# Stored right operands of two square projections: sums formed in DRAM, ScalarE passes in a fixed order, and a later place for two products

## The chip, the cores and the metric

The kernel runs on one core of a Trainium2 chip. The metric is the device time of one execution in microseconds. A core has TensorE (PE in the profile; PEld is its weight load), VectorE (DVE), ScalarE (ACT), GpSimd (POOL) and SyncE (SP), each with its own queue of instructions that it takes in order, and 16 DMA engines that move data between DRAM and the on-chip SBUF. DMAs of this kernel are issued by SP or by POOL; only POOL issues those that add to what stands at the destination (`accum_op=ALU.add`).

## The reference

One decoder layer on x of 1024 tokens by 1024 features, all in float32:

```python
h = _layer_norm(ALPHA * h + 0.5 * _swiglu(h, ffn1_w_gate, ffn1_w_up, ffn1_w_down), ...)
mix = _token_mixers(h, w_in, ...)        # [HGRN2 recurrence ; spatial gating] @ w_out
h = _layer_norm(ALPHA * h + mix, ...)
xa = _memory_cross_attention(h, mem, ...)  # softmax(q k^T) v @ xa_w_o, 256 memory tokens
h = _layer_norm(ALPHA * h + xa, ...)
h = _layer_norm(ALPHA * h + 0.5 * _swiglu(h, ffn2_w_gate, ffn2_w_up, ffn2_w_down), ...)
```

`_swiglu` is `(silu(x @ w_gate) * (x @ w_up)) @ w_down` with an inner width of 2816. The two square matrices of this case are `w_out` (1024 x 1024, the mixers' output) and `xa_w_o` (1024 x 1024, the attention's output).

## The kernel before

Every product is made of three matmuls on operands split in two: `split` makes a hi part on ACT (a Copy that rounds) and a lo part on DVE (raw minus hi), and `mm3` (L133 to L137) multiplies hi by hi (L135), lo by hi (L136) and hi by lo (L137). Weights come through `load_split`: SP loads a raw tile (tag `raw`, three buffers, L121), ACT writes hi (L112), DVE writes lo (L113). Hi tiles have the tag `whi` with six buffers, lo tiles `wlo` with five.

The large products are done by Strassen's scheme, with seven half-size products in place of eight. In the FFNs the gate and up projections run through `st_g` and `st_u` (names end in f1 or f2 for the two FFNs; the profile writes f), then the down projection through `dp`. The two square projections are done by the class `Square`: its seven products p = 1 to 7 have on their right a block of the matrix or a sum of blocks (5 = 11+12, 6 = 5+22, 4 = 6+21, 7 = 22+12, and 1, 2, 3 are the blocks 11, 21, 22), each in two halves n of 512 KB, and each half in a hi and a lo part. These 14 right operands of each matrix are not made when they are needed. `prepare_square` makes them ahead, while the first FFN runs, and stores them in DRAM (`sq_mx` for w_out, `sq_xa` for xa_w_o), from where `Square.fetch` loads them later (`sh_` and `sl_` tiles).

Before, an operand goes through these steps: a raw tile `pre` (one buffer for all) is loaded by SP (L234), or, for a sum, POOL adds the next block from DRAM onto the same tile (L236). ACT writes hi (`ph`, L239) and its negative (`pl`, L240), POOL adds the raw tile onto `pl` by a DMA, which leaves lo (L241), SP stores hi (L242) and POOL stores lo (L243). Twelve raw tiles are loaded by SP, sixteen are accumulated.

What sets the order: the preparation is a generator (a flow) that yields numbers of microseconds. `spawn` starts a flow, and `tick(us)`, called after each piece of FFN or mixer work, lowers its count and lets it go on at zero. `prepare_square` runs from `later`, first for w_out and then for xa_w_o. The flows set the order in which the program is written; a scheduler then sets the order on each engine, and an engine keeps that order on the chip.

At the end of the token mixers there are two halves of 512 tokens (`m0`, `m1`). `body` gives the units of a half: gates and `us` units with the heads' recurrences started between them, and four `vs` units. `tail` gives four gate units (`ps_wg`); behind each the head outputs are transposed (`pt_oa`), the other group's stored result is loaded back (`mx_again`, L1231) and both are added (`s_mx`, L1047), which makes the left operand of the output projection. `msq` is that projection: products 2 (`sx2_mx`) and 1 (`sx_mx`) need only the first token half, product 7 and those after it (`sy_mx` among them) need both.

Of the kernel before, what the change touches and what calls it, by code (L numbers as in the profile page):

```python
# [20 lines left out]
HALF = T // 2  # L21
# [5 lines left out]
ALPHA = 2.0 ** 0.25  # L27
EPS = 1e-5
WARM = 32
LEVELS = [64, 32, 16, 8, 4, 2, 1]  # L30


@with_exitstack
def hybrid_layer_kernel(ctx: ExitStack, tc: tile.TileContext, a, out):
    nc = tc.nc
# [4 lines left out]
    wpool = ctx.enter_context(tc.tile_pool(name="wpool", bufs=5))  # L40
# [3 lines left out]
    dram = ctx.enter_context(tc.tile_pool(name="dram", bufs=1, space=bass.MemoryType.DRAM))  # L44
# [70 lines left out]
    def load_raw(view, name, pool=None):  # L115
        if pool is not None:
            raw = pool(f"{name}_r", [P] + list(view.shape[1:]))
            nc.sync.dma_start(raw, view)
            return raw
        raw = wpool.tile([P] + list(view.shape[1:]), F32, tag="raw", bufs=3, name=f"{name}_r")  # L120
        nc.sync.dma_start(raw, view)  # L121
        return raw

# [87 lines left out]
    def layer_norm(y, gb, bb, name):  # L211

        stt = sm(f"st_{name}", [P, 2, 6])
        for j in range(2):
# [3 lines left out]

    SUMS = {1: ["11"], 5: ["11", "12"], 6: ["11", "12", "22"], 4: ["11", "12", "22", "21"],
            2: ["21"], 3: ["22"], 7: ["22", "12"]}

    def prepare_square(w, ops, name):


        wv = w.rearrange("(kb n i p) (db d) -> kb n db p i d", kb=2, n=2, i=2, p=P, db=2)
        for n in range(2):
            raw = None
            for p, blocks in SUMS.items():  # L230
                b = wv[int(blocks[-1][0]) - 1, n, int(blocks[-1][1]) - 1]
                if len(blocks) == 1:
                    raw = wpool.tile([P, 2, HALF], F32, tag="pre", bufs=1, name=f"pre_{name}_{n}{p}")
                    nc.sync.dma_start(raw, b)  # L234
                else:
                    nc.gpsimd.dma_start(raw, b, accum_op=ALU.add)  # L236
                hi = wpool.tile([P, 2, HALF], F32R, tag="whi", bufs=6, name=f"ph_{name}_{n}{p}")
                lo = wpool.tile([P, 2, HALF], F32R, tag="wlo", bufs=5, name=f"pl_{name}_{n}{p}")
                nc.scalar.activation(hi, raw, AF.Copy)  # L239
                nc.scalar.activation(lo, hi.bitcast(F32), AF.Copy, scale=-1.0)  # L240
                nc.gpsimd.dma_start(lo, raw, accum_op=ALU.add)  # L241
                nc.sync.dma_start(ops[p - 1, n, 0], hi.bitcast(F32))  # L242
                nc.gpsimd.dma_start(ops[p - 1, n, 1], lo.bitcast(F32))  # L243
                yield 13

    class Square:

# [711 lines left out]
    class Mixers:  # L959
# [251 lines left out]
        def body(self):  # L1211
            start = [[partial(spawn_late, self.recurrence, h)] for h in range(H)]
            vs = token_units(self.half, 2560, "wvs", self.evac_v)
            return (start[0] + self.gates(1) + self.us(0) + self.us(1) + start[1] + self.gates(2)
                    + self.us(2) + self.us(3) + start[2] + self.gates(3) + vs[:2] + start[3] + vs[2:])

# [6 lines left out]
    def play(units):  # L1223
        for unit in units:
            unit()
            if not (isinstance(unit, partial) and unit.func is spawn_late):
                tick(5.2)
# [13 lines left out]
    play(m1.body())  # L1241


    msq.fetch(2, 1)
    x = msq.bank("sx2")
    for n in range(2):
# [2 lines left out]
    x = msq.bank("sx")  # L1249
    for n in range(2):  # L1250
        msq.step(1, x, 0, 0, n, True)
    play(m1.tail())
    msq.fetch(7)
    msq.gb, msq.bb = load_bc(a["ln2_g"][0], a["ln2_b"][0], "mx")
    for t in range(4):
# [179 lines left out]
```

## Time and profile before

| | before |
|---|---|
| median of 3 runs | 2135.43 us (2132.91 to 2135.46) |
| profiled execution | 2131.09 us |
| its span | 2129.3 us |
| mean granted PE clock | 0.976 |
| PE busy | 2029.2 us, 95% |
| DVE busy | 1492.0 us, 70% |
| ACT busy | 931.6 us, 44% |
| POOL busy | 166.8 us, 8% |
| q1 (SP's DMA queue) | 338.82 MB, 47.3% of 16 engines' span |
| q0 (POOL's DMA queue) | 37.75 MB, 7.9% |

The stages, by the first matmul of each: the memory's K and V projections to about 63 us, FFN1's gate and up to 553.5 us, FFN1's down to about 770 us, the mixers and their output projection to about 1245 us, cross-attention to about 1505 us, and FFN2 to the end (its gate and up to 1907.4 us). The busy time of an engine excludes its register, branch, semaphore and DMA-issuing instructions, except that POOL's DMA instructions appear in the timeline with the time that POOL spent on them. A DMA is shown by the time from its issue to its landing.

### The profile page before, as it was taken

To read this page: it belongs to the slowest core of one execution; us is meant where nothing else is said; L and a number is where in the kernel's file an instruction comes from. 1 tells how busy PE (TensorE), PEld (TensorE's weight loads), DVE (VectorE), ACT (ScalarE), POOL (GpSimd) and SP (SyncE) were. 2 spreads that over 40 slices of the span, in tenths; PEclk is the share of its full clock that TensorE was granted. 3 is DMA by queue.
4 is the path that set the end of the run, shared out by engine and by line. 5 is a ranking of instruction groups with operands and counts; after the bars stand their busy time and mean duration, and the time that the engine had idled before them with its cause. 6 is when DMAs were issued, how large, how long until landed. Compare 5 with 4: busy or idle time off the path is not lost.

```text
span 2129.3 us, 25517 instructions
## 1 busy us (share of the span) xinstructions
PE 2029.2 (95%) x9550; PEld 1688.8 (79%) x9550; DVE 1492.0 (70%) x2240; ACT 931.6 (44%) x1311; POOL 166.8 (8%) x224
## 2 busy tenths in 40 slices
PE   8999898998899999999996979999999999999998
PEld 7787686777788888888885868887888888888886
DVE  5866564756767876776773774469777677676688
ACT  6643343434443547746642434335432333334432
POOL 0111111111000220100010110002000000000011
PEclk9999899999999999999998989999999999999999
DMA  8588777877878752133225533455223233268874
GB/s 282 161 226 234 206 224 207 233 191 245 289 279 284 272 164 89 41 109 109 80 98 226 191 117 92 168 197 179 83 85 120 94 99 124 81 225 283 279 272 170
DMA packets 267420, 378.20 MB, mean 178 GB/s; under 512 B 16544, under 2 KB 156448, under 8 KB 267296
## 3 DMA queue, kind: packets, MB, share of 16 engines
q1 hardware_dynamic: 254880, 338.82, 47.3%
q0 software_dynamic: 12416, 37.75, 7.9%
q8 instruction: 75, 1.23, 0.2%
q14 instruction: 49, 0.40, 0.1%
HBM read 257.51 MB, written 104.33 MB: 170 GB/s over the span
## 4 chain that ended last, share of the span: by engine, by line
PE 68%; DVE 3%; DMA 1%; issue 1%; POOL 0%; ACT 0%; POOLq 0%; SPq 0%; DVEq 0%; ACTq 0%
PE dp_f L135 6%; PE dp_f L136 6%; PE dp_f L137 6%; PE st_uf L136 3%; PE st_gf L136 3%; PE st_gf L137 3%; PE st_uf L137 3%; PE st_uf L135 3%; PE st_gf L135 3%; PE psl L1119 2%; PE paq L135 1%; PE paq L136 1%; PE paq L137 1%; PE sx_mx L135 1%; PE ps_wu L135 1%; PE sx_mx L136 1%
## 5 line engine op out<-in xcount | busy, mean ns | idle before, releaser
L135 PE MATMUL dp_f<-wd_f_h,ah_f 128*128 128x512 f32 x552 | 209.9, 393 | 7.0 <-ACT ah_f L112 7.0
L136 PE MATMUL dp_f<-wd_f_l,ah_f 128*128 128x512 f32 x552 | 214.6, 392 | 0.2 <-DVE wd_f_l L113 0.2
L137 PE MATMUL dp_f<-wd_f_h,al_f 128*128 128x512 f32 x552 | 206.0, 390 | 0.1
L135 PEld LDWEIGHTS dp_f<-wd_f_h,ah_f 128*128 128x128 f32 x552 | 104.4, 189 | 29.3 <-ACT ah_f L112 7.8
L136 PEld LDWEIGHTS dp_f<-wd_f_l,ah_f 128*128 128x128 f32 x552 | 104.4, 189 | 22.3 <-DVE wd_f_l L113 0.7
L137 PEld LDWEIGHTS dp_f<-wd_f_h,al_f 128*128 128x128 f32 x552 | 103.6, 188 | 21.8 <-DVE al_f L113 0.5
L112 ACT ACTIVATE wd_f_h<-wd_f_r 128x1024 fp32r<-128x1024 f32 x72 | 73.2, 1021 | 94.3 <-DVE wd_f_r L587 31.7
L112 ACT ACTIVATE ah_f<-ar_f 128x1024 fp32r<-128x1024 f32 x72 | 73.4, 1020 | 67.7 <-DMA ar_f<-lops 65.5
L113 DVE TENSOR_TENSOR al_f<-ar_f,ah_f 128x1024 fp32r<-128x1024 f32 x72 | 84.5, 1174 | 23.9 <-ACT ah_f L112 23.5
L113 DVE TENSOR_TENSOR wu_f_l<-wu_f_r,wu_f_h 128x1024 fp32r<-128x1024 f32 x44 | 53.7, 1219 | 60.3 <-ACT wu_f_h L112 38.9
L113 DVE TENSOR_TENSOR wg_f_l<-wg_f_r,wg_f_h 128x1024 fp32r<-128x1024 f32 x44 | 53.6, 1219 | 56.0 <-ACT wg_f_h L112 52.7
L113 DVE TENSOR_TENSOR wd_f_l<-wd_f_r,wd_f_h 128x1024 fp32r<-128x1024 f32 x72 | 84.2, 1174 | 9.9 <-ACT wd_f_h L112 9.9
L135 PE MATMUL st_uf<-xh,wu_f_h 128*128 128x512 f32 x168 | 68.7, 409 | 17.3 <-DVE top_gf L467 14.1
L135 PE MATMUL st_gf<-xh,wg_f_h 128*128 128x512 f32 x168 | 66.8, 398 | 5.5 <-ACT wg_f_h L112 5.5
L137 PE MATMUL st_uf<-xh,wu_f_l 128*128 128x512 f32 x168 | 68.2, 406 | 1.1 <-DVE wu_f_l L113 1.1
L136 PE MATMUL st_uf<-xl,wu_f_h 128*128 128x512 f32 x168 | 68.0, 405 | 0.0
L137 PE MATMUL st_gf<-xh,wg_f_l 128*128 128x512 f32 x168 | 66.9, 398 | 1.1 <-DVE wg_f_l L113 1.1
L136 PE MATMUL st_gf<-xl,wg_f_h 128*128 128x512 f32 x168 | 66.6, 396 | 0.0
L711 POOL TENSOR_SCALAR nm_f<-nm_f 128x1 f32<-128x1 f32 x8 | 7.3, 917 | 753.0 <-ACT xl L710 753.0
L112 ACT ACTIVATE wu_f_h<-wu_f_r 128x1024 fp32r<-128x1024 f32 x44 | 46.2, 1050 | 29.4 <-issue 12.8
L112 ACT ACTIVATE wg_f_h<-wg_f_r 128x1024 fp32r<-128x1024 f32 x44 | 46.2, 1051 | 28.9 <-PE st_gf L136 15.5
L135 PEld LDWEIGHTS st_uf<-xh,wu_f_h 128*128 128x128 f32 x168 | 33.3, 198 | 26.2 <-issue 14.5
(522 smaller groups left out, 5987.6 us busy)
## 6 DMA issues: line engine op xcount, KB each, us to landing
ar_f<-lops SPq DMA_DIRECT2D x66, 512.0 KB, 5.1
wd_f_r<-in_ffn_w_down_dram SPq DMA_DIRECT2D x56, 512.0 KB, 4.7
wg_f_r<-in_ffn_w_gate_dram SPq DMA_DIRECT2D x44, 512.0 KB, 4.2
wu_f_r<-in_ffn_w_up_dram SPq DMA_DIRECT2D x44, 512.0 KB, 4.2
lops<-bot_gf SPq DMA_DIRECT2D x21, 512.0 KB, 2.8
lops<-top_uf SPq DMA_DIRECT2D x21, 512.0 KB, 3.0
lops<-bot_uf SPq DMA_DIRECT2D x21, 512.0 KB, 4.8
waq_r<-in_xa_w_q_dram SPq DMA_DIRECT2D x16, 512.0 KB, 3.7
```

What stands on the lines that cost most here:

```text
L112: order(nc.scalar.activation(hi, src, AF.Copy))
L113: order(nc.vector.tensor_tensor(lo, src, hi.bitcast(F32), op=ALU.subtract))
L135: nc.tensor.matmul(ps, lh, rh, start=first, stop=False, skip_group_check=more)
L136: nc.tensor.matmul(ps, lh, rl, start=False, stop=False, skip_group_check=more)
L137: nc.tensor.matmul(ps, ll, rh, start=False, stop=last, skip_group_check=more)
L711: nc.gpsimd.tensor_scalar(nmean, nmean, -1.0 / D, None, op0=ALU.mult)
L1119: nc.tensor.matmul(psl[:m, (i * NC2 + c) * 64:(i * NC2 + c + 1) * 64] .rearrange("p (n b) -> p n b", b=B), e[:, :m], blk(e, B)[:, :, 1, :] ...
```

## The change

- The sums of blocks are no longer formed in SBUF. For each matrix four sums (5, 7, 6, 4) are formed in DRAM: a copy of two halves, and two accumulating DMAs that add the second block, from DRAM to DRAM. POOL issues all of them: 16 copies and 16 accumulations for both matrices.
- Each operand has a flow of its own, `operand`. POOL loads the raw tile (it now takes the tag `raw`, which has four buffers in place of three; the tag `pre` is gone), ACT writes hi and its negative (both with the tag `whi`; the preparation has no `wlo` tile any more), and POOL stores both. Then POOL adds the raw block to the stored negative, from DRAM to DRAM, which leaves lo in `sq_`. `tc.keep_in_program_order` fixes the two ACT passes against the other pinned instructions. The order of the products is 1, 7, 4, 6, 5, 2, 3, and a new operand starts every 13 us of the flow's count. SP has no part in it.
- In the second token half the four `vs` units come after the last recurrence is started; before, two stood ahead of it. The four gate units of `m1.tail` come before products 2 and 1 of w_out; before, they came after them.

```diff
+RAW = 4
...
-        raw = wpool.tile([P] + list(view.shape[1:]), F32, tag="raw", bufs=3, name=f"{name}_r")
+        raw = wpool.tile([P] + list(view.shape[1:]), F32, tag="raw", bufs=RAW, name=f"{name}_r")
...
-        for n in range(2):
-            raw = None
-            for p, blocks in SUMS.items():
-                b = wv[int(blocks[-1][0]) - 1, n, int(blocks[-1][1]) - 1]
-                if len(blocks) == 1:
-                    raw = wpool.tile([P, 2, HALF], F32, tag="pre", bufs=1, name=f"pre_{name}_{n}{p}")
-                    nc.sync.dma_start(raw, b)
-                else:
-                    nc.gpsimd.dma_start(raw, b, accum_op=ALU.add)
-                hi = wpool.tile([P, 2, HALF], F32R, tag="whi", bufs=6, name=f"ph_{name}_{n}{p}")
-                lo = wpool.tile([P, 2, HALF], F32R, tag="wlo", bufs=5, name=f"pl_{name}_{n}{p}")
-                nc.scalar.activation(hi, raw, AF.Copy)
-                nc.scalar.activation(lo, hi.bitcast(F32), AF.Copy, scale=-1.0)
-                nc.gpsimd.dma_start(lo, raw, accum_op=ALU.add)
-                nc.sync.dma_start(ops[p - 1, n, 0], hi.bitcast(F32))
-                nc.gpsimd.dma_start(ops[p - 1, n, 1], lo.bitcast(F32))
+        wb = w.rearrange("(kb k) (db d) -> kb db k d", kb=2, db=2)
+        sums = {}
+        for p, first, b in ((5, "11", "12"), (7, "22", "12"), (6, 5, "22"), (4, 6, "21")):
+            sums[p] = dram.tile([HALF, HALF], F32, name=f"sum_{name}{p}")
...
+            for rows in halves:
+                nc.gpsimd.dma_start(sums[p][rows], src[rows])
+            yield 6
+            for rows in halves:
+                nc.gpsimd.dma_start(sums[p][rows], add[rows], accum_op=ALU.add)
+            yield 6
...
+        for p in (1, 7, 4, 6, 5, 2, 3):
+            for n in range(2):
+                spawn(operand(sums[p][2 * n * P:2 * (n + 1) * P].rearrange("(i p) d -> p i d", p=P),
+                              ops[p - 1, n], f"{name}_{p}{n}"))
                 yield 13
+
+    def operand(src, dst, name):
+        raw = wpool.tile([P, 2, HALF], F32, tag="raw", bufs=RAW, name=f"pr_{name}")
+        nc.gpsimd.dma_start(raw, src)
+        yield 10
+        hi, neg = (wpool.tile([P, 2, HALF], F32R, tag="whi", bufs=6, name=f"p{i}_{name}") for i in "hn")
+        tc.keep_in_program_order(nc.scalar.activation(hi, raw, AF.Copy))
+        tc.keep_in_program_order(nc.scalar.activation(neg, hi.bitcast(F32), AF.Copy, scale=-1.0))
+        nc.gpsimd.dma_start(dst[0], hi.bitcast(F32))
+        nc.gpsimd.dma_start(dst[1], neg.bitcast(F32))
+        yield 9
+        nc.gpsimd.dma_start(dst[1], src, accum_op=ALU.add)
...
+            if self.half:
+                return (start[0] + self.gates(1) + self.us(0) + self.us(1) + start[1] + self.gates(2)
+                        + self.us(2) + self.us(3) + start[2] + self.gates(3) + start[3] + vs)
...
+    play(m1.tail())
     msq.fetch(2, 1)
...
-    play(m1.tail())
     msq.fetch(7)
```

Where the instructions move to is set by the scheduler. POOL at the program's start, before (`mem` names are the layer norm of the memory tokens, in two tiles of 128):

```order
L89 MEMSET ident_75 128x128
L97 MEMSET mhalf_113 128x16
L913 MEMSET ones_5843 128x128
L90 ISA
L90 AFFINE_SELECT ident_75<-ident_75 128x128
L183 TENSOR_SCALAR ve_mem0_172<-mv_mem0_166 128x1
L186 TENSOR_TENSOR rs_mem0_167<-ve_mem0_172,mhalf_113 128x1
L802 TENSOR_SCALAR nm_mem0_168<-mv_mem0_166 128x1
L803 TENSOR_TENSOR nm_mem0_168<-nm_mem0_168,rs_mem0_167 128x1
```

POOL at the same place after:

```order
L98 MEMSET mhalf_113 128x16
L233 DMA sum_mx5_1019<-in_w_out_dram 256x512 x2
L91 ISA
L91 AFFINE_SELECT ident_75<-ident_75 128x128
L233 DMA sum_mx7_1108<-in_w_out_dram 256x512 x2
L233 DMA sum_xa5_2844<-in_xa_w_o_dram 256x512 x2
L233 DMA sum_xa7_2943<-in_xa_w_o_dram 256x512 x2
L925 MEMSET ones_5899 128x128
L184 TENSOR_SCALAR ve_mem0_172<-mv_mem0_166 128x1
L236 DMA sum_mx5_1019<-in_w_out_dram 256x512 x2
L187 TENSOR_TENSOR rs_mem0_167<-ve_mem0_172,mhalf_113 128x1
L814 TENSOR_SCALAR nm_mem0_168<-mv_mem0_166 128x1
```

Eight copies and then the accumulations stand between the steps of the memory norm; the other sums follow behind it, ahead of the first operand's load. In the middle of FFN1, POOL's queue before:

```order
L236 DMA pre_mx_01_1019<-in_w_out_dram 128x2x512
L241 DMA pl_mx_05_1114<-pre_mx_01_1019 128x1024
L243 DMA sq_mx_121<-pl_mx_05_1114 128x1024
L236 DMA pre_mx_01_1019<-in_w_out_dram 128x2x512
L241 DMA pl_mx_06_1229<-pre_mx_01_1019 128x1024
L243 DMA sq_mx_121<-pl_mx_06_1229 128x1024
```

and after:

```order
L253 DMA sq_mx_121<-ph_mx_70_1675 128x1024
L248 DMA pr_mx_40_1812<-sum_mx4_1310 128x2x512
L254 DMA sq_mx_121<-pn_mx_70_1676 128x1024
L256 DMA sq_mx_121<-sum_mx7_1108 256x1x512
L253 DMA sq_mx_121<-ph_mx_71_1791 128x1024
L248 DMA pr_mx_41_1919<-sum_mx4_1310 128x2x512
L254 DMA sq_mx_121<-pn_mx_71_1792 128x1024
L256 DMA sq_mx_121<-sum_mx7_1108 256x1x512
```

The raw tile of an operand is loaded while the operand two places ahead of it is being stored. The last six operands (`xa_50`, `51`, `20`, `21`, `30`, `31`) now have their ACT passes among those of the down projection; before, all passes of the preparation stood in the gate and up stage. At the mixers' end, SP's queue before (`sh_`, `sl_` are the operands fetched for product 7, 4 and 6; the second digit is the half n):

```order
L268 DMA sl_mx_70_8961<-sq_mx_121 128x1024
L268 DMA sh_mx_71_8964<-sq_mx_121 128x1024
L268 DMA sl_mx_71_8965<-sq_mx_121 128x1024
L268 DMA sh_mx_40_9057<-sq_mx_121 128x1024
L268 DMA sl_mx_40_9058<-sq_mx_121 128x1024
L268 DMA sh_mx_41_9061<-sq_mx_121 128x1024
L268 DMA sl_mx_41_9062<-sq_mx_121 128x1024
L268 DMA sh_mx_60_9065<-sq_mx_121 128x1024
L268 DMA sl_mx_60_9066<-sq_mx_121 128x1024
L1231 DMA mx_again00_8939<-oa_124 128x1024
```

and after:

```order
L280 DMA sl_mx_70_9034<-sq_mx_121 128x1024
L1246 DMA mx_again00_8937<-oa_124 128x1024
L280 DMA sh_mx_71_9037<-sq_mx_121 128x1024
L280 DMA sl_mx_71_9038<-sq_mx_121 128x1024
L280 DMA sh_mx_40_9113<-sq_mx_121 128x1024
L280 DMA sl_mx_40_9114<-sq_mx_121 128x1024
L280 DMA sh_mx_41_9117<-sq_mx_121 128x1024
L1246 DMA mx_again01_8941<-oa_124 128x1024
```

The first load of `mx_again` moves ahead of most of these fetches. On PE products 2 and 1 now follow the gate units of the tail, with the transposes `pt_oa` between their matmuls.

More of the change, by code (lines that the diff above doesn't have):

```diff
@@ new lines, in prepare_square @@
+        wb = w.rearrange("(kb k) (db d) -> kb db k d", kb=2, db=2)
+        sums = {}
+        for p, first, b in ((5, "11", "12"), (7, "22", "12"), (6, 5, "22"), (4, 6, "21")):
+            sums[p] = dram.tile([HALF, HALF], F32, name=f"sum_{name}{p}")
+            src = sums[first] if first in sums else wb[int(first[0]) - 1, int(first[1]) - 1]
+            add = wb[int(b[0]) - 1, int(b[1]) - 1]
+            halves = [slice(i * 2 * P, (i + 1) * 2 * P) for i in range(2)]
+            for rows in halves:
[4 more added lines that the diff above has]
+            yield 6
@@ new lines, in prepare_square @@
+        for p, b in ((1, (0, 0)), (2, (1, 0)), (3, (1, 1))):
+            sums[p] = wb[b[0], b[1]]
+        for p in (1, 7, 4, 6, 5, 2, 3):
+            for n in range(2):
+                spawn(operand(sums[p][2 * n * P:2 * (n + 1) * P].rearrange("(i p) d -> p i d", p=P),
+                              ops[p - 1, n], f"{name}_{p}{n}"))
+                yield 13
+    def operand(src, dst, name):
[9 more added lines that the diff above has]
+        nc.gpsimd.dma_start(dst[1], src, accum_op=ALU.add)
```

3 lines of the change are left out of this document (removed).

## The prediction

> **What bounds the kernel now.** The page is read first: busy times, the slices, the chain.
>
> ```profile
> PE 2029.2 (95%) x9550; PEld 1688.8 (79%) x9550; DVE 1492.0 (70%) x2240; ACT 931.6 (44%) x1311; POOL 166.8 (8%) x224
> PE   8999898998899999999996979999999999999998
> DMA  8588777877878752133225533455223233268874
> PE 68%; DVE 3%; DMA 1%; issue 1%; POOL 0%; ACT 0%; POOLq 0%; SPq 0%; DVEq 0%; ACTq 0%
> ```
>
> TensorE is the bound of the whole span, and no instruction of it is removed. So the change can only touch the 5% in which PE is not busy and the stretches in which its clock is low. The slices (53 us each) put those at the start, through the first FFN (to slice 11) and in slices 22 and 24. The windows view prices the stages (columns: length, then busy time of PE, PEld, DVE, ACT and POOL, the granted PE clock, DMA share, GB/s).
>
> ```profile
> 0.00:63.00 63.00, 53.97 (x361) 49.57 (x362) 38.33 (x64) 39.45 (x84) 3.33 (x16) 0.95 0.87 277
> 63.00:153.00 90.00, 86.51 (x377) 71.07 (x375) 71.03 (x89) 52.03 (x72) 11.30 (x13) 0.98 0.66 179
> 153.20:553.50 400.30, 360.94 (x1513) 291.91 (x1511) 251.00 (x328) 157.00 (x192) 49.32 (x59) 0.95 0.79 222
> 553.50:640.00 86.50, 86.46 (x372) 71.43 (x373) 61.80 (x66) 40.56 (x43) 0.00 (x0) 0.97 0.85 296
> 640.00:770.00 130.00, 130.00 (x592) 107.41 (x592) 106.86 (x125) 56.00 (x69) 18.16 (x17) 1.00 0.74 254
> 1152.00:1176.00 24.00, 9.04 (x24) 6.73 (x25) 16.26 (x24) 4.12 (x4) 0.00 (x0) 0.50 1.00 400
> 1564.70:1907.40 342.70, 342.70 (x1513) 283.86 (x1512) 249.08 (x324) 115.56 (x145) 0.00 (x0) 1.00 0.35 116
> ```
>
> Rows three and seven are the same gate and up work of the two FFNs, 1513 matmuls each. The second FFN prepares nothing beside it and takes 342.7 us; the first takes 400.3. The difference, 57.6 us, is the most that a better preparation can return in that stage: 39.4 us of PE idle (400.30 - 360.94) and 18.2 us of slower matmuls at a clock of 0.95. What the preparation does there is in the views of waits, first of the engines, then of SP's DMA queue, then of PE alone between 153 and 554 us (total, times, longest).
>
> ```profile
> ACT ph_xa L239 <- DMA pre_xa<-in_xa_w_o_dram: 74.8, 11, 14.9
> ACT ph_mx L239 <- DMA pre_mx<-in_w_out_dram: 69.3, 12, 15.4
> ...
> SPq L242 <- ACT ph_mx L239: 72.4, 13, 16.3
> SPq L242 <- ACT ph_xa L239: 70.4, 12, 16.9
> ...
> PE st_uf L135 <- DVE top_gf L467: 14.1, 3, 8.0
> ```
>
> ACT stands 144.1 us before the hi pass of an operand, waiting for its raw tile, and SP as long before the store of it. Both run in order, so what is queued behind stands too. One place shows how that reaches PE (timeline; the bracket is the idle time before):
>
> ```profile
> 210.25 1.06 ACT L239 ACTIVATE ph_mx<-pre_mx 128x1024 fp32r<-128x1024 f32 x1 [15.42 <-DMA pre_mx<-in_w_out_dram]
> 211.21 1.04 ACT L112 ACTIVATE wu_f_h<-wu_f_r 128x1024 fp32r<-128x1024 f32 x1
> ...
> 212.30 0.50 PE L135 MATMUL st_uf<-xh,wu_f_h 128*128 128x512 f32 x1 [1.80 <-ACT wu_f_h L112]
> ```
>
> The weight split wu_f_h is ready long before, but stands behind ph_mx for 15.42 us, and PE runs dry. The raw tile is late since it is formed by accumulating into itself: the next block is added only after the hi, neg and lo steps of the last one have read it.
>
> **The change part by part.** Prices of a 512 KB transfer come from POOL's queue in four short stretches, each holding one of them: 205.9 to 209.4 (a block added from DRAM), 215.0 to 218.3 (SBUF added to SBUF), 202.0 to 204.2 (a plain store); the last figure is the share of 16 engines.
>
> ```profile
> q0 software_dynamic: 269, 0.52, 82.2%
> ...
> q0 software_dynamic: 144, 0.52, 96.2%
> ...
> q0 software_dynamic: 144, 0.52, 64.0%
> ```
>
> Share times length: 3.5 x 0.822 = 2.88 us, 3.3 x 0.962 = 3.17 us, 2.2 x 0.64 = 1.41 us of all 16 engines.
>
> *A. The start.* The sums are 16 copies and 16 accumulations of 512 KB, and the new order puts all of them at the head of POOL's queue, beside the loads of mem, x, wk and wv, with the memory norm's small steps between. A copy from DRAM to DRAM is not in the trace; nearest is the plain store, 1.41 us. An accumulation from DRAM to DRAM is not either; nearest is the one from DRAM, 2.88. 16 x 1.41 + 16 x 2.88 = 68.6 us of DMA time. Free in 0 to 63 us are 0.13 x 63 = 8.2 us, in 63 to 153 us 0.34 x 90 = 30.6 us. In the second stretch five operands of before go: each two stores and an SBUF accumulation (2.82 + 3.17 = 5.99), with a plain load (two of them) or an accumulating one (three); 5 x 5.99 + 2 x 1.41 + 3 x 2.88 = 41.4 us. So over 0 to 153 us the sums find 8.2 + 30.6 + 41.4 = 80 us: lower bound 0. Upper bound: all of them overtake the first loads, 68.6 - 8.2 = 60 us. In between, POOL's first eight copies (11.3 us) and, at half of the engines up to 63 us, some 20 us of accumulations fall on the loads; less 8.2 makes 23. POOL's queue adds a little of its own, because the memory norm stands between those DMAs:
>
> ```profile
> 8.93 0.19 POOL L803 TENSOR_TENSOR nm_mem<-nm_mem,rs_mem 128x1 f32<-128x1 f32 x1
> ...
> 200.97 1.21 POOL L236 DMA_DIRECT2D pre_mx<-in_w_out_dram  x1
> ```
>
> Eight copies at between 0.57 and 1.21 us of POOL and three accumulations at 1.21 stand ahead of that last norm step: it moves from 9 to about 17 us. PE waits for it before its first K product, but the loads are late then too, so I count 2 us. A: +25, between 0 and +60.
>
> *B. FFN1's gate and up.* Gone are the shared raw tile, the chain through it, and SP's 40 DMAs with the waits behind L242; the hi and neg passes are pinned behind loads that POOL issues about two operands ahead. ACT keeps two passes per operand (1.06 us each), so no busy time goes. An operand now costs a load, two stores and an accumulation in DRAM: 3 x 1.41 + 2.88 = 7.1 us of DMA. 23 operands stood in 153 to 553 us at 7.4 or 8.9 us (5.99 plus the load), about 190 us; now some 22, 156 us. DMA in that stage falls from 0.79 x 400 = 316 to 282 us, 0.82 of a 343 us stage, so no bound by itself. Two waits can remain: raw tiles now come from the weights' own tag (four buffers for both, three before for the weights alone), and hi and neg take two of the six hi buffers where they took one. A DMA share above 0.8 also means bursts. I take 90% of the 57.6 us: B = -52, between -61 (all, with the 3.5 us of PE idle in 63 to 153) and -30.
>
> *C. FFN1's down.* In the new order the last six operands of w_o stand between the splits of the down projection, where before there were none (POOL has no entry in 553 to 640). That is 6 x 7.1 = 43 us of DMA into stretches at 0.85 and 0.74, which have 13.0 and 33.8 us free. Below nothing is excluded, for nothing is taken out there. If the spare time could all be used: 0. If only the first stretch's could: 43 - 13 = 30. ACT is in order there as well, and its splits stand for the loads already:
>
> ```profile
> ACT ah_f L112 <- DMA ar_f<-lops: 65.5, 38, 5.8
> ```
>
> With half of the six in each stretch the first lacks 21 - 13 = 8 us; I add 6 us for the clock after gaps of a few us. C: +14, between 0 and +30.
>
> *D. The mixer's end.* The stall there is in three gaps of PE:
>
> ```profile
> 1159.23 1.94 PE L1038 MATMUL pt_oa<-ident,ot 128*128 128x128 f32 x8 [11.58 <-DVE s_mx L1047]
> ...
> 1167.38 0.79 PE L135 MATMUL sy_mx<-sh_mx,xh 128*128 128x512 f32 x1 [6.22 <-ACT xh L112]
> ...
> 1170.97 0.80 PE L135 MATMUL sx_mx<-sh_mx,xh 128*128 128x512 f32 x1 [1.51 <-DVE r_mx L304]
> ...
> 1148.03 10.61 DMA mx_again<-oa
> ```
>
> They sum to 19.3 us, and the 9.04 us of PE work in 1152 to 1176 ran at 0.50, which is 4.5 us more: 23.8 us at stake. Two causes: the load mx_again lands 10.6 us after its issue behind a burst of prefetches (share 1.00), and the products 2 and 1 of w_out (48 matmuls each) were used up before it. Now the load's issue stands ahead of product 7's second half and all of product 4, and both products run behind the gate units: 48 matmuls at 342.7 / 1513 = 0.227 us are 10.9 us, about the load's time, and product 1 covers the xh wait. Left over I put 8 us, for the pairs wait for one another and the share stays at 1.00: D = -16, between -23.8 and -6 (if the load merely moves with the burst).
>
> *At nothing.* The four units of the mixer's vs move by one place in a stretch where PE is busy throughout; the dropped lo tiles free space that nobody waited for; the second stall, at 1233 to 1245 us, has other producers. If that cover went, PE would wait for at most one unit, 24 matmuls or 5.4 us.
>
> Sum: 25 - 52 + 14 - 16 = -29. The profiled execution took 2131.09 us, so 2102.1; the median of the runs, 2135.43, stands 4.3 us above it, and my number is on the median's scale: 2106.
>
> **A rule against it.** The row first: 0.87 busy at 277 GB/s in the first 63 us with POOL's queue empty. The Trainium skill, page "DMA: Bandwidth & Descriptors", section "Issuing engines are not separate DMA queues", says that transfers started by different engines end up on the same 16 DMA engines and interleave, so that issuing from another engine saves sequencer time alone. By that, moving the stores to POOL returns only their issue, and the sums at the start are paid in full; the sum would be A = +60, and this is the first rival. The trace agrees so far that both queues run in one share; whether half of the engines go to each, no run here shows yet.
>
> **The rivals.**
> *1. Slower, at the start.* The sums take the engines from the loads one for one: A = +60, and C = +30 by the same crowding, with B and D as above: 2131.1 + 60 + 30 - 52 - 16 = 2153, 2157 on the median's scale. For it: 0.87 of the engines is already used in 0 to 63 us, and the sums stand first in POOL's queue. Against: 80 us of room by 153 us, and POOL waits between its DMAs. It decides from where A + C passes 52 + 16 = 68 us.
> *2. The waits move.* ACT now stands before pinned passes whose raw tile comes late, since POOL must see each neg store land before it adds to it, and the next load stands behind. Then B is -30 with A and C as forecast: 2131.1 + 25 - 30 + 14 - 16 = 2124, or 2128: still faster, by 0.3%; with D at -6 it is 2138, within 0.2%.
> *3. Hidden sums.* The sums fit in the free time and the down phase hides its six: A = 5, C = 0, B = -58, D = -20: 2058, 2062.
> *4. Nothing happens in FFN1:* the weights' split was late for the DMA share's sake, not for ACT's order. Against it stand the rows at 210 to 212 us. It would be +25 + 14 - 16 over before: 2158.
>
> **How the numbers follow.** The forecast (net between -60 and -15) has 0.40; rivals 1 and 4 together 0.30; rival 2 0.18, of it 0.10 within 0.2%; rival 3 0.12. A change of 0.2% (4.3 us, as much as the spread between the profiled run and the median) is about what can be told from none. Faster: 0.40 + 0.08 + 0.12 = 0.60; same 0.10; slower 0.30. The range leaves out half of rival 3 and the worse third of rival 1: 2066 to 2160. The forecast's own range is 2075 to 2120.
>
> **What would show it.** Right would be: ph_mx and ph_xa gone from the waits, or under 40 us in all; 18 halves of gate and up in 343 to 355 us at a clock of 0.99 or more; at the start the DMA share at 1.0 and the first st_gf 20 to 30 us later; in the down phase PE idle of about 10 us; at the mixer's end gaps under 8 us in all. The prediction falls if the DMA share stays above 0.95 past 200 us, if PE waits for raw tiles' splits in the gate and up stage as before, or if the start loses over 45 us.

## The result, and the profile after

The changed kernel takes 2156.04 us (median of 3 runs, 2152.73 to 2161.2) against 2135.43: ratio 1.0103, 95% interval 1.0069 to 1.0137. It is about 21 us slower, where 29 us faster was forecast. Its profiled execution has a span of 2154.0 us, 24.7 more than the span before. The page of the changed kernel, busy times and slices:

```profile
PE 2025.3 (94%) x9550; PEld 1684.8 (78%) x9550; DVE 1490.3 (69%) x2240; ACT 932.4 (43%) x1311; POOL 217.8 (10%) x296
PE   2899999999778999999999979999999999999997
PEclk6999999999999999999999989999999999999999
DMA  9985789568999764213325633445223233267874
```

PE has the same matmuls. Two holes are new: the first slice (2 tenths busy, clock 6) and the slices of the first FFN's down projection (7, 7, 8, with DMA at 9). The windows view of the changed kernel, cut at the first matmul of each stage (columns as in the prediction):

```profile
0.00:63.00 63.00, 22.43 (x148) 21.13 (x149) 15.14 (x26) 13.33 (x22) 12.91 (x29) 0.70 0.91 255
192.80:552.50 359.70, 345.50 (x1514) 284.64 (x1513) 242.72 (x322) 156.29 (x188) 63.62 (x87) 0.99 0.79 230
552.50:711.00 158.50, 130.93 (x528) 103.10 (x528) 86.49 (x90) 67.79 (x71) 17.17 (x23) 0.94 0.96 319
994.30:1264.70 270.40, 252.77 (x1336) 213.90 (x1334) 196.92 (x411) 136.23 (x198) 31.89 (x40) 0.97 0.43 150
```

In 0 to 63 us PE does 22.4 us of work, where it did 54.0. The table puts every microsecond of the difference in a stage. Boundaries are the starts of single matmuls in the timeline: the first of the last 18 gate and up halves, the first `dp_f`, the first gate unit (`ps_wg`) of the mixers' second stretch, the first `paq` of attention, and the first gate matmul of FFN2.

| stage | before | after | difference | forecast |
|---|---|---|---|---|
| start, up to the 18 halves | 153.2 | 192.8 | +39.6 | A: +25 |
| FFN1 gate and up, 18 halves | 400.3 | 359.7 | -40.6 | B: -52 |
| FFN1 down and mixers' first part | 404.8 | 441.8 | +37.0 | C: +14 |
| mixers' second part | 287.0 | 270.4 | -16.6 | D: -16 |
| attention | 260.4 | 260.4 | 0 | 0 |
| FFN2 | 623.6 | 628.9 | +5.3 | 0 |
| span | 2129.3 | 2154.0 | +24.7 | -29 |

At the start PE waits for one thing, the memory norm (the `mem` tiles that ScalarE writes). Its wait for that from 0 to 153 us before and from 0 to 193 us after (total, times, longest):

```profile
PE ptm L811 <- ACT mem L804: 3.1, 2, 2.0
```

```profile
PE ptm L823 <- ACT mem L816: 35.5, 2, 29.1
```

That is 32.4 of the 39.6 us. POOL's timeline of the changed kernel (start, length, engine, line, operation; the bracket is the idle time before it), then ACT's and PE's:

```profile
1.39 1.44 POOL L233 DMA_DIRECT2D sum_mx<-in_w_out_dram  x2 [0.35 <-issue]
3.16 0.59 POOL L233 DMA_DIRECT2D sum_mx<-in_w_out_dram  x1
10.05 0.57 POOL L233 DMA_DIRECT2D sum_mx<-in_w_out_dram  x1 [6.30 <-issue]
...
20.36 0.26 POOL L184 TENSOR_SCALAR ve_mem<-mv_mem 128x1 f32<-128x1 f32 x1
23.88 1.03 POOL L236 DMA_DIRECT2D sum_mx<-in_w_out_dram  x1 [3.26 <-issue]
34.54 0.91 POOL L236 DMA_DIRECT2D sum_mx<-in_w_out_dram  x1 [9.63 <-issue]
35.14 0.93 POOL L187 TENSOR_TENSOR rs_mem<-ve_mem,mhalf 128x1 f32<-128x1 f32 x1
...
36.63 0.19 POOL L815 TENSOR_TENSOR nm_mem<-nm_mem,rs_mem 128x1 f32<-128x1 f32 x1
```

```profile
36.86 1.24 ACT L816 ACTIVATE mem<-mem,nm_mem,rs_mem 128x1024 f32<-128x1024 f32 x1 [29.72 <-POOL nm_mem L815]
...
38.15 0.69 PE L823 MATMUL ptm<-ident,mem 128*128 128x128 f32 x2 [29.09 <-ACT mem L816]
```

`ve_mem` stood behind the eight copies: it ran at 20.36 us, and at 6.11 in the kernel before. `rs_mem` is a step of under 1 us, ready from 20.6 us on. Between it and `ve_mem` stand two accumulations, and POOL sits 3.26 and 9.63 us before them, waiting for nothing that the profile names, until it can issue them. What it waits for is the landing of earlier DMAs of its queue. The first copy, issued at 1.39 us, and the first accumulation, issued at 23.88, landed after (the view of `sum_mx`, cut to each of the two)

```profile
DMA to landing us min/median/max: 8.3/8.3/8.3
...
DMA to landing us min/median/max: 10.3/10.3/10.3
```

so at 9.7 and 34.2 us, and the fourth copy was issued at 10.05, the second accumulation at 34.54: each 0.3 us behind a landing. So it is for all thirteen sum DMAs from 10.05 to 84.07 us, and the copies have nothing in the program to wait for. VectorE stood idle from 7.4 us on, so it held nothing up. Those brackets are what POOL pays for a DMA when earlier ones of its queue are still under way; the 1.21 us of an accumulation in the trace of before, which the prediction used, is the price behind a single store.

The down stage of the changed kernel, its waits of PE from 552 to 800 us (total, times, longest), where before had one of 6.0 us. In both kernels the first of these waits (9.5 us here, the 6.0 before) is for the first down product, and so belongs to the stage ahead by the boundaries of the table:

```profile
PE dp_f L136 <- ACT ah_f L113: 29.4, 13, 9.5
PE dp_f L136 <- ACT dt_f L741: 6.9, 1, 6.9
```

In 552.5 to 711 us PE is idle for 27.6 us, and its 528 matmuls take 130.9 us at a mean clock of 0.94. At the rate of the kernel before (686 in the 157.5 us from 553.5) they would take 121; the idle time and the slower matmuls together make the 37 us.

### The profile page after: what moved, and what is told of

The parts are those of the page before. It is cut to its first block, busy times and chain, and to the rows that moved or that the text cites. A ratio compares the mean times of both kernels' runs of the same rounds, so it can differ in the third digit from the quotient of the medians.

```text
span 2154.0 us, 25546 instructions
## 1 busy us (share of the span) xinstructions
PE 2025.3 (94%) x9550; PEld 1684.8 (78%) x9550; DVE 1490.3 (69%) x2240; ACT 932.4 (43%) x1311; POOL 217.8 (10%) x296
## 4 chain that ended last, share of the span: by engine, by line
PE 76%; DMA 10%; DVE 7%; issue 3%; ACT 2%; POOL 1%; SPq 0%; DVEq 0%; POOLq 0%; ACTq 0%
PE st_gf L138 6%; PE st_gf L137 6%; PE st_gf L136 6%; PE st_uf L138 6%; PE st_uf L136 6%; PE st_uf L137 6%; DMA ar_f<-lops 3%; PE dp_f L137 3%; PE dp_f L136 3%; PE dp_f L138 3%; DMA wd_f_t<-rops 2%; PE psl L1131 2%; PE paq L136 1%; PE paq L137 1%; PE paq L138 1%
## 5 line engine op out<-in xcount | busy, mean ns | idle before, releaser
L138 PE MATMUL dp_f<-wd_f_h,al_f 128*128 128x512 f32 x552 | 190.6, 391 | 1.6 <-DVE al_f L114 1.5
L136 PEld LDWEIGHTS dp_f<-wd_f_h,ah_f 128*128 128x128 f32 x552 | 105.3, 192 | 67.4 <-ACT ah_f L113 36.6
L138 PEld LDWEIGHTS dp_f<-wd_f_h,al_f 128*128 128x128 f32 x552 | 104.0, 189 | 24.7 <-DVE al_f L114 2.9
L113 ACT ACTIVATE wg_f_h<-wg_f_r 128x1024 fp32r<-128x1024 f32 x44 | 46.3, 1052 | 32.4 <-PE st_gf L137 17.1
L479 DVE TENSOR_TENSOR top_uf<-bot_uf,st_uf 128x512 f32<-128x512 f32 x21 | 14.4, 687 | 62.5 <-PE st_uf L138 52.2
L114 DVE TENSOR_TENSOR wu_f_l<-wu_f_r,wu_f_h 128x1024 fp32r<-128x1024 f32 x44 | 53.7, 1220 | 1.8 <-ACT wu_f_h L113 1.8
```

The costliest lines, as they stand in the source:

```text
L113: order(nc.scalar.activation(hi, src, AF.Copy))
L114: order(nc.vector.tensor_tensor(lo, src, hi.bitcast(F32), op=ALU.subtract))
L136: nc.tensor.matmul(ps, lh, rh, start=first, stop=False, skip_group_check=more)
L138: nc.tensor.matmul(ps, ll, rh, start=False, stop=last, skip_group_check=more)
L479: nc.vector.tensor_tensor(t0, b0, product(2), op=ALU.add)
```

## The experiments

Ratios are to the kernel before on the same chip, with a 95% interval. Its median was 2135.4 to 2136.8 us on all the chips used, so times from different chips are set side by side. Lengths of stages are from one profile of each kernel.

**The start: POOL's queue or the DMA engines' share.** All 32 sum DMAs stay at the start, but behind the memory norm on POOL:

```diff
-                nc.gpsimd.dma_start(sums[p][rows], src[rows])
+                tc.keep_in_program_order(nc.gpsimd.dma_start(sums[p][rows], src[rows]))
...
-                nc.gpsimd.dma_start(sums[p][rows], add[rows], accum_op=ALU.add)
+                tc.keep_in_program_order(nc.gpsimd.dma_start(sums[p][rows], add[rows], accum_op=ALU.add))
```

The sums of both matrices are formed one after the other here, with their pauses (48 us each) ahead of each matrix's operands, so that the operands keep their places.

> The changed kernel with all 32 sum DMAs still at the start, but pinned in program order on POOL behind the last step of the memory norm (they start some 9 us into the span). Theory of the queue: PE stood 29 us for the memory norm since its small POOL steps were queued behind DMAs that POOL could not issue; with the norm ahead of them the first gate and up product starts less than 15 us later than in the kernel before (39.6 us later in the changed one), and the kernel takes 2156 - 27 = 2129 us (2122 to 2136). Theory of the share: the sums' bytes crowd the loads of wk, x and wv, whoever is first in POOL's queue; then at least 30 us of the 39.6 stay and the kernel takes 2146 or more.

Measured: 2121.22 us, ratio 0.9932 (0.991 to 0.9953). The time is just below the queue theory's range. The 18 halves start at 158.5 us, 5.3 later than before and 34.3 earlier than in the changed kernel; all other stages are as there (359.4, 443.7, 269.8, 258.6, 628.6). PE's wait for the norm is 2.8 us. POOL's timeline and the first window:

```profile
9.00 0.19 POOL L815 TENSOR_TENSOR nm_mem<-nm_mem,rs_mem 128x1 f32<-128x1 f32 x1
9.13 1.45 POOL L230 DMA_DIRECT2D sum_mx<-in_w_out_dram  x2
17.53 1.00 POOL L233 DMA_DIRECT2D sum_mx<-in_w_out_dram  x1 [6.95 <-DMA sum_mx<-in_w_out_dram]
26.86 0.90 POOL L233 DMA_DIRECT2D sum_mx<-in_w_out_dram  x1 [8.33 <-issue]
```

```profile
0.00:63.00 63.00, 49.37 (x325) 45.68 (x325) 32.18 (x54) 34.40 (x76) 11.54 (x27) 0.89 1.02 309
```

POOL is blocked as before (8.33 us), but nobody waits for it. The DMA engines are full, 1.02 against 0.87 before, and that costs 5 us, not the 23 put down to it. The queue theory holds. One thing moves along with it: the copies now come behind the first loads (SP has issued the last load of x by 22.0 us, by 31.7 in the changed kernel). With the copies first and only the norm's steps early, part of the 34 us might have been lost to late loads; that was not tried apart.

**The mixers' edit alone**, on the kernel before, and the changed kernel without it (the later place of the `vs` units belongs to it, as in the diff of the change):

```diff
...
+    play(m1.tail())
     msq.fetch(2, 1)
...
-    play(m1.tail())
     msq.fetch(7)
```

> The kernel before with the mixers' new order alone (vs units after the last recurrence, gate units ahead of products 2 and 1). The stage from the mixers' first gate unit to the first attention projection took 16.6 us less in the changed kernel. Theory: that comes from this edit alone, so this kernel takes 2135.4 - 16.6 = 2119 us (2115 to 2123), with the pt_oa wait of 11.6 us gone and everything up to the mixers as before. Rival: the gain there hangs on the operands' part of the change (another DMA load at that time, or four raw buffers), and this kernel is within 5 us of before.

> The changed kernel with the mixers' order of the kernel before. If the mixers' edit is worth the same beside the other edits: 2156 + 16.6 = 2173 (2168 to 2178), with the second part of the mixers at 287 us (270.4). In the run of that edit alone the stage from the first down product to the mixers' second half took 413.6 us against 404.8; if the edit costs that, here the stage is 9 us shorter (433) and the time 2164; if that was chance, the stage stays at 438 to 445.

Measured: alone 2121.13 us, ratio 0.9938 (0.9914 to 0.9962), the mixers' second part 270.1 us; without it 2172.54, ratio 1.0173 (1.0149 to 1.0197), second part 285.6, the down stretch 444.9. Both times are as forecast. The edit is worth 14.5 us alone and 16.5 beside the rest by the medians, 16.8 and 15.2 by the stage, and the 9 us that its own run showed in the down stretch do not belong to it. What is left of the gaps in the changed kernel (PE's waits, 1120 to 1200 us):

```profile
PE sx_mx L136 <- DVE r_mx L316: 3.4, 1, 3.4
PE sx_mx L136 <- issue: 1.3, 1, 1.3
PE pt_oa L1050 <- DVE s_mx L1059: 0.3, 1, 0.3
```

**The down stage: the six late operands.** First, a spacing of 10 in place of 13, which moves all of their ScalarE passes ahead of the down projection:

```diff
-                yield 13
+                yield 10
```

> The changed kernel with a new operand every 10 us of the flow in place of 13, so that the last operand's ScalarE passes stand ahead of the first split of the down projection. Theory: the 37 us lost in the first FFN's down stage are the six operands in it; they go (0 to 6 us left), the gate and up stage takes up to 10 us more, and the kernel takes 2156 - 37 + 5 = 2124 us (2119 to 2135). Rival: the same transfers crowd the gate and up stage instead and PE waits there for weights; then 30 us come back and the kernel is at 2145 to 2156. Second rival: the down stage is slow for another reason (SP's order, four raw buffers): its loss stays above 20 us.

Measured: 2168.99 us, ratio 1.0158 (1.014 to 1.0176): slower still, which no theory had said. The down stretch falls to 419.1 us (441.8), but the gate and up stage rises to 395.5:

```profile
193.40:588.90 395.50, 357.98 (x1514) 291.18 (x1512) 242.32 (x323) 168.76 (x200) 79.21 (x108) 0.95 0.82 240
...
347.27 1.06 ACT L113 ACTIVATE wu_f_h<-wu_f_r 128x1024 fp32r<-128x1024 f32 x1 [9.15 <-DMA sq_mx<-ph_mx]
```

At this place the weight's hi tile waits for the landing of a `ph` store, from which it takes its buffer, and the store stands in POOL's queue. That this is what close spacing costs was refuted later: with the stores on SP it costs as much (see below, under a better version). Second, the stores and accumulations of the six left out, their ScalarE passes kept:

```diff
+        if name[:4] in ("xa_5", "xa_2", "xa_3"):
+            return
         nc.gpsimd.dma_start(dst[0], hi.bitcast(F32))
...
+                        q = 1 if self.name == "xa" and p in (5, 2, 3) else p
```

> The changed kernel with the stores and the accumulation of the six late operands (5, 2 and 3 of xa_w_o) left out; their loads and their two ScalarE passes stay at the same places, and the products use the stored operand 1 in their stead, so the result is another but the work on PE is the same. Per operand 1.4 of 7.1 us of DMA stay. Theory of the DMA share: the down stage lost 37 us because its DMA engines were full (0.99); here at most 12 us of loss stay and the kernel takes 2156 - 28 = 2128 us (2122 to 2136). Rival, ScalarE's order: the pinned passes stand before late raw tiles and hold the splits of the down projection behind them; then at least 25 us of the loss stay, and the kernel takes 2144 or more.

Measured: 2132.43 us, ratio 0.998 (0.9965 to 0.9995). The down stretch takes 423.7 us, so 18 of the 37 us go with the DMAs: more loss stays than the first theory allowed (12), less than the rival's 25. The passes alone, at the same places on ScalarE, do not hold it. The loads of the stage (`ar_f`) took 6.0 us to land at the median, 7.0 in the changed kernel and 4.9 before. The six raw tiles still take buffers here, and SP waits 8.2 us in all for their hi passes before it can load a weight; whether that makes the rest was not tried apart. The 19 that stay led to a second profile of the kernel before:

> The kernel before, unchanged, for a second profile of it. From the first product of the first FFN's down projection to the mixers' second half the profile of before took 404.8 us, the mixers' edit alone 413.6, and kernels that hold no operand's ScalarE passes there 419 to 421. If the 404.8 was at the low end of what executions of before spread over, here it is 408 to 415, and of the 37 us lost there in the changed kernel some 5 to 9 are chance; if it is 403 to 407 again, they are not.

Measured: 2135.67 us, ratio 0.9998 (0.998 to 1.0016), span of its profiled execution 2138.6. The down stretch takes 414.7 us here. Its waits of PE from 553 to 960 us, where the first profile had one of 6.0:

```profile
PE dp_f L135 <- ACT ah_f L112: 9.7, 3, 7.3
PE dp_f L135 <- DVE db_f L734: 3.1, 1, 3.1
```

So that stretch differs by 10 us between two profiles of the same kernel, and the one that the prediction was made on is the shorter. Against 414.7 the six operands cost 27 us (and the 19 that stayed are 9), and kernels without operands there (419.1, and 421.3 below) are within 7 us of before.

**Which queue stores.** The changed kernel with the stores on SP:

```diff
-        nc.gpsimd.dma_start(dst[0], hi.bitcast(F32))
-        nc.gpsimd.dma_start(dst[1], neg.bitcast(F32))
+        nc.sync.dma_start(dst[0], hi.bitcast(F32))
+        nc.sync.dma_start(dst[1], neg.bitcast(F32))
```

> The changed kernel with the hi and neg stores issued by SP in place of POOL; all else the same. Theory: for the gate and up stage it does not matter which queue issues them as long as no wait stands in it, since the raw tiles come early; the stage stays at 355 to 365 us, the start and the down stage as in the changed kernel, and the time is 2156 (2148 to 2162). Rival: SP's relief was a good part of the 40 us won in that stage (SP stood 143 us for the hi passes in the kernel before); then the stage goes back by 15 us or more and the time is 2170 or more. Second rival: POOL's blocked issue holds the tiles of hi and neg too long; with SP's stores the stage or the down stage gets 5 to 15 us shorter, 2141 to 2150.

Measured: 2149.18 us, ratio 1.006 (1.0042 to 1.0078). The gate and up stage takes 347.6 us, 12 less, at the clock and nearly the length of the second FFN's (342.7):

```profile
192.80:540.40 347.60, 342.88 (x1514) 283.63 (x1512) 240.32 (x318) 156.96 (x188) 38.19 (x42) 1.00 0.80 233
```

The second rival's outcome came. How much it won is less sure: with POOL's stores the stage took 359.7 us in the changed kernel, 359.4 with the sums behind the norm, but 353.7 in the run with the mixers' old order, where this stage is the same; with SP's it took 347.6, 347.0 and 346.3 in three runs. So taking the stores from SP was no gain; it cost 6 to 13 us here. The down stretch takes 9 back (450.6), and the kernel's time is 7 us below the changed one's. The reason is seen in part: ScalarE waits 15.4 us in that stage of the changed kernel for stores to land, 8.5 here. With the sums behind the norm as well:

> The sums pinned behind the memory norm (2121 us measured for that alone) and in addition the stores issued by SP. With POOL left to loads and accumulations only. If the stores on POOL cost nothing: 2121 (2116 to 2127). If POOL's blocked issue costs in the down stage (its loss was 39 us with the stores on POOL): 2100 to 2112. If SP's waits come back: 2135 or more.

Measured: 2110.88 us, ratio 0.9879 (0.9851 to 0.9908); start 159.6, gate and up 347.0, down 445.3. The time is in the second case's span, but the gain came in the gate and up stage, not in the down stage that the expectation named.

**The flow's count between load and passes.** In the changed kernel:

```diff
-        yield 10
+        yield 0.1
         hi, neg = ...
```

> The changed kernel with the ScalarE passes of an operand right behind the issue of its load (the flow's count of 10 us between them set to 0.1), still pinned. Theory: what the gate and up stage won is the lead of the load over the pinned passes; without it ScalarE stands for the load, some 5 to 8 us per operand, the weight splits stand behind it, and the stage takes 385 us or more (359.7 in the changed kernel, 400.3 before): 2180 us or more. Rival: the gain comes from ending the chain through one raw tile and SP's blocked queue; the scheduler's order and four raw buffers hide the load anyway, and the kernel stays within 10 us of 2156.

Measured: 2156.05 us, ratio 1.0086 (1.0063 to 1.0108); gate and up 352.6. The rival holds: the count in the flow is not what hides the load. In the changed kernel ScalarE's passes of an operand have no wait for a raw tile in that stage, only four for buffers or PE, of 1.6 us at most. But the edit did not take the lead away: the first load was issued at 150.6 us and its hi pass ran at 186.1 (153.9 and 196.3 in the changed kernel), and the shortest lead of the 28 is 14.9 us (19.3). So the scheduler's order keeps it, and what a kernel without any lead would lose is not shown. ScalarE stood 144 us for raw tiles before, 129 of them in this stage; that they went with the one shared raw tile and its chain is argued, not tried apart.

**Raw buffers.** `RAW = 3` in the changed kernel:

> The changed kernel with three raw buffers in place of four. The second FFN took 628.9 us in the changed kernel and 626 to 631 in all others with four buffers, against 623.6 and 623.9 in the two with three, though nothing was changed there. Theory: four buffers make the scheduler write SP's loads of the down projections in another order, which costs 5 us in the second FFN and 5 to 10 in the first one's down stage; here the second FFN is back at 624, the first FFN's down and the mixers' first part at 430 to 437 (441.8), the gate and up stage at most 5 us longer, and the time is 2145 (2138 to 2152). Rival: three buffers for weights and operands starve the gate and up stage (359.7 us): 10 us or more are lost there and the time is 2160 or more.

Measured: 2187.59 us, ratio 1.0243 (1.021 to 1.0276); start 201.2, gate and up 377.4, down 448.6, FFN2 626.3. The rival holds: the fourth buffer is worth 31 us, 18 of them in the gate and up stage. FFN2 is not back at 624, and the 5 us there stay unexplained (623.6 and 625.2 in the two profiles of before, 624.0 with the mixers' edit alone, 626.0 to 630.8 in all with the new operands).

**Toward a better version.** Both have the sums behind the norm and the stores on SP. First the close spacing (`yield 10`), then 13 with the pause between the matrices dropped:

```diff
...
         yield from prepare_square(a["w_out"][0], sq_ops["mx"], "mx", mx)
-        yield 48
         yield from prepare_square(a["xa_w_o"][0], sq_ops["xa"], "xa", xa)
```

> Sums behind the memory norm, stores by SP, and a new operand every 10 us of the flow in place of 13. The last showed (with POOL's stores) the gate and up stage 36 us longer, and a weight split that waited 9.2 us for the landing of a hi store: theory, hi tiles are shared and were held by stores stuck in POOL's queue. With SP issuing them the tiles come free in time: gate and up within 8 us of 360, the down stage's loss under 20 us, and the kernel takes 2121 - 20 = 2101 us (2092 to 2110), faster than all so far. Rival: it is the DMA engines' share and POOL's accumulations that can't go faster than one operand per 13 us, whoever stores: the gate and up stage is again 20 us or more longer and the kernel takes 2125 or more.

> Sums behind the memory norm and stores by SP (2110.9 us measured), and the flow's pause of 48 us between the operands of the two matrices dropped, so that only three of xa_w_o's operands are left in the down stage, at the same spacing of 13 us. Theory: the down stage loses about 3 us for each operand in it; 10 us come back (445.3 to 435), the gate and up stage stays within 5 us of 347, and the time is 2103 (2096 to 2108). Rival: the pause let POOL catch up, and without it the gate and up stage fares as with a spacing of 10 us (382.8): 2120 or more.

Measured: the first 2118.74 us, ratio 0.9926 (0.9902 to 0.995), gate and up 382.8, down 421.3. The second 2097.91, ratio 0.9825 (0.9805 to 0.9845), gate and up 346.3, down 429.8; it beats both kernels, by 39 and 58 us, and it came as forecast. The first did not: its gate and up stage is 35.8 us longer than at a spacing of 13 (347.0), as much as with POOL's stores (395.5 against 359.7), so stores stuck in POOL's queue are not what close spacing costs. The stage is as the rival said, the time 6 us below it. The down stretch follows the number of operands in it: 421.3 us with none, 429.8 with three, 445.3 with six. The gate and up stage of each:

```profile
158.00:540.80 382.80, 354.43 (x1513) 289.02 (x1512) 239.61 (x322) 167.38 (x200) 49.91 (x55) 0.97 0.86 251
```

```profile
158.20:504.50 346.30, 342.90 (x1513) 283.60 (x1511) 242.85 (x322) 162.24 (x194) 47.15 (x52) 1.00 0.90 263
```

The 0.86 is a mean over a stretch with operands and a pause without. Cut at the pause, and beside it the same stretch of the second kernel:

```profile
158.00:333.00 175.00, 161.15 (x680) 130.94 (x679) 102.75 (x139) 78.10 (x93) 25.47 (x28) 0.96 0.92 262
333.00:383.00 50.00, 50.00 (x223) 41.39 (x222) 39.57 (x53) 15.32 (x21) 1.98 (x4) 1.00 0.44 137
```

```profile
158.00:333.00 175.00, 175.00 (x774) 144.91 (x773) 123.10 (x164) 81.04 (x98) 24.25 (x27) 1.00 0.89 260
```

In the pause the first kernel's PE is never idle; while operands come every 10 us it does 680 matmuls in 175 us, at a share of 0.92 and 262 GB/s, where the second does 774 at 0.89 and 260. The shares are too near to tell the two apart. In the first, VectorE waits 52.4 and 45.5 us for gate and up weights to land, in the second 36.3 and 28.8:

```profile
DVE wg_f_sa L448 <- DMA wg_f_r<-in_ffn_w_gate_dram: 52.4, 7, 11.1
DVE wu_f_sa L448 <- DMA wu_f_r<-in_ffn_w_up_dram: 45.5, 7, 8.6
```

```profile
DVE wg_f_sa L448 <- DMA wg_f_r<-in_ffn_w_gate_dram: 36.3, 8, 9.0
DVE wu_f_sa L448 <- DMA wu_f_r<-in_ffn_w_up_dram: 28.8, 5, 6.6
```

The loads of `wu_f_r` between 158 and 333 us land 11.1 us after their issue at the median in the first, 6.0 in the second. So either the operands' transfers crowd out the weights' at that pace, or operands at 10 us hold two of the four raw buffers most of the time, as with three buffers; the two were not tried apart.

## Why the prediction was wrong, step by step

The forecast was a gain of 29 us, and the span grew by 24.7: the sum is off by 53.7 us. Of these, C has 23.0, A 14.6, B 11.4 and FFN2 5.3, and D gives 0.6 back. No one term turns the sign: with A as measured the sum is -14, with C as well +9, with B as well +20.

**A, the start (+25; measured +39.6): the step whose mechanism failed.** The prediction saw that eight copies and three accumulations would stand ahead of the last norm step, priced them at POOL's issue time, 0.57 to 1.21 us each, and moved the step from 9 to 17 us, at a cost of 2 us "since the loads are late then too". The step came at 43.4 us, the first of the two tiles at 36.6. POOL could not issue the next DMA until earlier ones had landed, so it stood up to 9.6 us before one. The 23 us put down to crowded engines are 5 in the run that has the same DMAs behind the norm, and the 2 us put down to the queue are 34 (with the order of the first loads, which that run moves too): the two terms were the wrong way round. That +25 is not further from 39.6 is luck, since one error, 32 too low, is partly made up by the other, 18 too high. The prediction weighed a rule of the Trainium skill here (page "DMA: Bandwidth & Descriptors", section "Issuing engines are not separate DMA queues"): the engines are shared, and another issuing engine saves only the time of issuing, which is usually small beside the DMA itself. The rival that went with it had A at +60; with the share at 1.02 the engines cost 5 us. The time of issuing itself was small here too, 0.56 to 1.03 us for one DMA; what cost 34 was the time that POOL stood before it could issue, with the norm's steps behind.

**B, gate and up (-52; -40.6).** The mechanism was right: ScalarE's waits for raw tiles are gone and PE's clock is at 0.99. The size fell short. With the stores on SP it is -52.7, but 6 us of the 12 between them are within what two runs of the same stage differ by. Of the 17 us that the stage still takes above the second FFN's, 9.5 are PE's wait for the first down product. Calling SP's 40 DMAs a relief was wrong in sign.

**C, down (+14, with +30 as its bound; +37, or +27 against the second profile of before): the step whose size failed most.** The six operands and their way of costing were seen: with four fifths of their DMA gone, half of the loss or more goes, and it follows their number. The +14 let the operands use all the free time of the stage, and the bound all of its first stretch's; but in the 158.5 us with the operands the share was 0.96 and the loads landed later, PE was idle for 27.6 us, and its matmuls, at a mean clock of 0.94, took 10 us more. The 8 us put down to waiting were 27.6, the 6 us for the clock 10. With none of the operands there the loss is within 7 us of the second profile of before.

**D, the mixers (-16; -16.6).** Right in place and size, and worth nearly the same with and without the rest. The `pt_oa` wait of 11.58 us, which the load and the two products were to cover, is down to 0.3.

**At nothing: FFN2 (+5).** Not foreseen, and its cause is open.

Of the rivals the first was nearest in kind: slower, 2157, by A + C over 68 us. The measured A + C is 76.6. That its time is within 1 us is chance: it had A at +60, C at +30 and B at -52. Its reason, engines taken from the loads, holds for little of A, as far as the run with the norm first shows; for C it has the loads' slower landing and the run without the stores on its side. "For it" the prediction named that the sums stand first in POOL's queue, which was the reason, and had priced that at 2 us. Rival 4 has 2158 as well, but with no gain in gate and up, which came.

## What to carry to other kernels

An engine that issues DMAs and also does small steps that others wait for must have those steps ahead of the DMAs in its queue. The scheduler put the copies, which wait for nothing, first, and a pin behind the last small step was worth 34 us here. Price a DMA that POOL issues with others of its queue under way at the landing of an earlier one, not at the issue time of a lone one. Work moved beside a bound engine needs room at the moment, not on average: the same stage took 36 us more when the operands came every 10 us and not every 13, at nearly the same DMA share, and a mean share over a stretch with a pause in it hides that.

## What the runs showed of the hardware that was not expected

POOL issued three 512 KB copies from DRAM to DRAM within 2.4 us and then none for 6.3 us. The accumulations that followed were issued 6.2 to 11.2 us apart up to 84 us, each 0.3 us after the landing of the one before (the first of them after that of a copy), with up to 10.3 us in which POOL did nothing else. SP's issues grew longer beside them as well: the first load of wk, the same DMA at the same place, took 2.91 us before and 5.65 after; in the run with the norm first, where no sum is under way yet, it took 2.87.

```profile
2.80 2.91 SPq L121 DMA_DIRECT2D wk_r<-in_xa_w_k_dram  x1
```

```profile
2.81 5.65 SPq L122 DMA_DIRECT2D wk_r<-in_xa_w_k_dram  x1
```

At the start three copies were under way at once, but no two of these accumulations. How many transfers POOL's queue holds, and whether bytes or rows count, was not settled.
